# Retention with increments from the last chunk down, and output gates multiplied on GpSimd during the attention

## The chip, the cores and the metric

The kernel runs on one core of a Trainium2 chip. The metric is the device time of one execution in microseconds, as the median of several runs. The engines are named as the profile names them: PE (TensorE matmuls and transposes; PEld are its weight loads), DVE (VectorE), ACT (ScalarE), POOL (GpSimd), and SP (SyncE), whose queue issues nearly all DMA transfers. Each engine works through a queue of its own in order and waits on semaphores for the others.

## What is computed

One inference step of a trunk of two layers over 1024 latent tokens and 256 context tokens, in float32, model width 1024. Each layer normalises and modulates the tokens, multiplies them with one input projection, and splits the result among three mixers and a gate path: bidirectional retention (4 heads, chunks of 128 tokens), grouped-query attention (6 heads), latent attention (6 heads). The mixers' outputs are joined, multiplied by SiLU of the gate, and go through the output projection into a gated residual:

```python
def step(s, inp):
    qi, ki, vi = inp
    a = jnp.einsum('bihd,bjhd->bhij', qi, ki) * intra
    o = (jnp.einsum('bhij,bjhe->bihe', a, vi)
         + jnp.einsum('bihd,bhde->bihe', qi, s) * q_dec[None, :, :, None])
    s = s * c_dec[None, :, None, None] + jnp.einsum('bjhd,bjhe->bhde', ki * k_dec[None, :, :, None], vi)
    return s, o

o_f, s_f = retention_chunkwise(q, k, v, log_g[0], s0_f)
o_b, s_b = retention_chunkwise(jnp.flip(q, 1), jnp.flip(k, 1), jnp.flip(v, 1), log_g[1], s0_b)
o = rms_norm(o_f + jnp.flip(o_b, 1))

y = jnp.concatenate([o_ret, o_gqa, o_mla], axis=-1) * jax.nn.silu(z_gate)
return x + g_res * (y @ w_out)
```

## The kernel before

The tokens are ten tiles of 128, eight latent (t = 0 to 7) and two context (8, 9). Matrix products with weights run as three matmuls each, on operands split into a high and a low part: wh and wl for weights (split on POOL, L195 and L196, from `raw`), ah and al for activations (`split_x`: ACT writes ah, L407, DVE subtracts it for al, L408). A layer goes through these stages:

- The input projection, in column blocks.
- The gate stage `z_blk` (L686 to L688): the last 1024 columns, transposed, with SiLU as tanh on ACT and (th + 1) z on DVE (`eo`, L693); the factor one half is left for later. Its results go to DRAM, `s_gT`, a row for each gate column. Between its matmul groups a generator `aside()` is stepped, which does the latents' keys and values, the retention, and the attention's preparation.
- The retention, over chunks. First, with t going up, `increments`: kd, the keys times the decay (two DVE multiplies, L804), four matmuls (L809), the forward state S[0:64] advanced on DVE (L816, L817), the backward increments copied by ACT into S[64:128]. Then a sweep over the tiles from the last to the first on DVE advances the backward state (L840, L841) and stores it (L842). Then three pipelined steps for each tile: `stage_a` multiplies q by the decay (qd, two DVE multiplies, L855), transposes it (L858), q and k (L864 and the line after), and copies them from PSUM (qdT and the block diagonal BD on ACT, kT on DVE, L869); `stage_b` is two matmuls (L875) and a multiply by the decay mask (At, L877); `stage_c` is eight matmuls (L884, L885), a norm, and a multiply into yx (L891).
- The attention (class `Attention`), in 60 passes a layer, each of a head pair's 256 queries. Scores (L1215, L1216, and for latent heads L1218), exponentials on ACT, transposes (L1256) with pT split by ACT (L1260) and DVE (L1261), products with V (L1272, L1273). POOL makes the query tiles Qg, Qm, Qr (L1137, L1139) and splits K and V; each `y_job`, 30 a layer, spreads the reciprocal sums on POOL (rb, L1303), transposes them on PE (L1306) and multiplies the heads on DVE (L1307).
- The output projection `phase_d`: for each tile `gated` transposes the retention's output (L1423), multiplies it and the heads by the gates and one half on DVE (L1424, L1425), reloads x into yx and splits the product; then 24 matmuls for each tile and column block of 256 (L259 to L261), the multiply by the residual gate (eg, L1451) and the residual add on POOL (L1453). Only the first of the four column blocks has `gated` in it.

Tiles are rotating buffers (`bufs=`): a new one waits until the readers of the old are done. The order on each engine is set by the program's text, by the generators' yields, and by a scheduler that places the instructions; `pin` holds an instruction in its place. Names: yx, the tokens' wide buffers, first q and head queries, then mixer outputs, then x; `gt`, the loaded gates; S, the retention states; cur and fin, the sweep's states; st and kpr, staged and final latent keys.

Of the kernel before, what the change touches and what calls it, by code (L numbers as in the profile page):

```python
# [10 lines left out]
F32 = mybir.dt.float32  # L11
# [9 lines left out]
NL = 8  # L21
# [56 lines left out]
RW = 1  # L78
PINV = 0
PINT = 0  # L80
# [4 lines left out]
def hybrid_trunk(tc, I, O):  # L85
# [315 lines left out]
    def pool_copy(o, i):  # L401
        G.tensor_scalar(o, i, 1.0, 1.0, op0=ALU.mult, op1=ALU.mult)
# [41 lines left out]
    def phase_b(l, p1, acts, ws, first, first_side, first_done, att):  # L444
# [267 lines left out]
        def aside():  # L712
# [30 lines left out]
    cdec_all = cst.tile([P, DEPTH, 4], F32, name="cdec")  # L743

# [8 lines left out]
    def decays(tmp):  # L753
# [22 lines left out]
        A.activation(cdec_all[0:64], lg_all[0:64, :, 0, :], AF.Exp, scale=128.0)  # L776
        A.activation(cdec_all[64:128], lg_all[64:128, :, 1, :], AF.Exp, scale=128.0)

    def retention(l, rt):
        if True:  # L780
            lg, dec, cdec = lg_all[:, l], dec_all[:, l], cdec_all[:, l]
            MT = rt.tile([P, 4, 128], F32, name="MT")
            dma(MT.rearrange("p h c -> p (h c)"), s_mt[l])

            def bc(ap, lo=0, hi=P):
                return ap.unsqueeze(2).to_broadcast([hi - lo, 4, 64])

            def h4(ap):
                return ap.rearrange("p (h d) -> p h d", h=4)

            S = rt.tile([P, NT, 256], F32, name="S")
            dma(S[0:64, 0, :].rearrange("p (h e) -> p h e", h=4), I["state_ret"][0, l, 0].rearrange("h d e -> d h e"))
            V.memset(S[0:64, NL, :], 0.0)
            fin = rt.tile([P, 256], F32, name="fin")

            def load(t):
                kv = rt.tile([P, 512], F32, name="kv", tag="kv", bufs=3)
                dma(kv, s_rkv[l][rows(t), :])
                return kv

            def increments(t, kv):
                kd = rt.tile([P, 4, 2, 64], F32, name="kd", tag="kd", bufs=1)
                for d in range(2):
                    i = V.tensor_tensor(kd[:, :, d, :], h4(kv[:, 0:256]), bc(dec[:, 2 + d, :]), op=ALU.mult)  # L804
                    if PINV and d == 0:
                        pin(i)
                ps = bank("m")
                for h in range(4):
                    i = T.matmul(ps[:, h * 64:(h + 1) * 64], kd[:, h, :, :].rearrange("p a b -> p (a b)"),  # L809
                             kv[:, 256 + h * 64:256 + (h + 1) * 64], start=True, stop=True)  # L810
                    if PINT and h == 0:
                        pin(i)

                if t != NL - 1:
                    nxt = S[0:64, t + 1, :] if t != NT - 1 else fin[0:64, :]
                    V.tensor_tensor(h4(nxt), h4(S[0:64, t, :]), bc(cdec[0:64, :], 0, 64), op=ALU.mult)  # L816
                    V.tensor_tensor(nxt, nxt, ps[0:64, :256], op=ALU.add)  # L817

                A.copy(S[64:128, t, :], ps[64:128, :256])

            kv = load(0)
            for _ in range(RW):
                yield
            for t in range(NT):
                yield
                nx_kv = load(t + 1) if t + 1 < NT else None
                increments(t, kv)
                kv = nx_kv
            for seq in (range(NL - 1, -1, -1), range(NT - 1, NL - 1, -1)):
                cur = rt.tile([P, 256], F32, name="cur", tag="cur", bufs=2)  # L830
                if seq[-1] == 0:
                    dma(cur[64:128, :].rearrange("p (h e) -> p h e", h=4), I["state_ret"][0, l, 1].rearrange("h d e -> d h e"))
                else:
                    V.memset(cur[64:128, :], 0.0)
                for t in seq:
                    last = t == seq[-1]
                    nx = None
# [6 lines left out]
                yield  # L844
            for d in range(2):
                dma(new_state[0, l, d].rearrange("h d e -> d h e"), fin[64 * d:64 * d + 64, :].rearrange("p (h e) -> p h e", h=4))

            BD = rt.tile([P, 2, 256], F32, name="BD")
            V.memset(BD, 0.0)

            def stage_a(t, kv):
                q = yx[t][:, 0:256]
                qd = rt.tile([P, 4, 2, 64], F32, name="qd", tag="kd", bufs=1)
                for d in range(2):
                    V.tensor_tensor(qd[:, :, d, :], h4(q), bc(dec[:, d, :]), op=ALU.mult)  # L855
                pt = bank("tp")
                for h in range(4):
# [4 lines left out]
                for j in range(2):  # L862
                    T.transpose(pt[:, j * 128:(j + 1) * 128], q[:, j * 128:(j + 1) * 128], ident)
                    T.transpose(pt[:, 256 + j * 128:256 + (j + 1) * 128], kv[:, j * 128:(j + 1) * 128], ident)  # L864
                pq = pt[:, 0:256].rearrange("p (j c) -> p j c", j=2)
                A.copy(BD[0:64, :, 0:128], pq[0:64])
                A.copy(BD[64:128, :, 128:256], pq[64:128])
# [785 lines left out]
```

## Time and profile before

| | before |
|---|---|
| median of 3 runs | 2179.33 us (2175.82 to 2180.6) |
| the profiled execution | 2173.39 us, span 2171.6 us |
| PE busy | 2095.2 us, 96% |
| DVE / ACT / POOL busy | 71% / 54% / 41% |
| retention, layer 0 / 1 | about 375 to 505 us / 1415 to 1550 us |
| attention, layer 0 / 1 | about 510 to 995 us / 1552 to 2040 us |
| output projection, layer 0 / 1 | about 996 to 1110 us / 2041 to 2168 us |

A line of groups reads: line, engine, operation, output from inputs, shapes, count, then busy time and the mean of one in ns, then the idle time of that engine just before these instructions and what ended it. A line of stretches gives its bounds and length, then the busy time and, in brackets, the number of instructions of PE, PEld, DVE, ACT and POOL in this order (or of PE alone where only PE was asked for), the clock granted to PE as a share of full speed, the share of DMA time, and GB/s.

### The profile page before, as it was taken

The page shows a single profiled execution, that of the slowest core. Times are in us where ns is not written, and L with a number is a line of the kernel's source. Part 1 is how long each engine was busy: PE and PEld are TensorE (multiplying, and loading weights), DVE is VectorE, ACT ScalarE, POOL GpSimd, SP SyncE. Part 2 cuts the span into 40 slices and gives each one's busy share as a digit, 9 for nine tenths or more (in the row PEclk, how much of TensorE's full clock was granted, in tenths as well). Part 3 has the DMA queues.
Part 4 walks back from the last instruction along what each step waited for, and adds up shares of the span by engine and source line. Part 5 has one row for each costly group of instructions (what it writes and reads, how often), then busy time and mean ns, then how long its engine had stood idle before and what let it go on. Part 6 is the DMA issues. An engine that isn't in the chain of part 4 may idle for free.

```text
span 2171.6 us, 42095 instructions
## 1 busy us (share of the span) xinstructions
PE 2095.2 (96%) x14928; PEld 1878.0 (86%) x14928; DVE 1546.4 (71%) x3982; ACT 1182.8 (54%) x3151; POOL 891.9 (41%) x1322
## 2 busy tenths in 40 slices
PE   6999999999999999998999999999999999999998
PEld 3899987787888888887999999888788888888898
DVE  4625683667989999998174358566699899999834
ACT  4503233226888888885253233313488888888523
POOL 2341242106475455423543224230465645544374
PEclk9999999999999999999999999999999999999999
DMA  9542436413010000026143112452301000000532
GB/s 323 144 140 61 127 110 197 122 49 99 12 39 17 11 22 16 10 63 179 49 153 105 46 58 52 152 151 71 91 23 27 17 22 22 16 5 18 178 95 98
DMA packets 196954, 173.15 MB, mean 80 GB/s; under 512 B 34968, under 2 KB 179208, under 8 KB 196744
## 3 DMA queue, kind: packets, MB, share of 16 engines
q1 hardware_dynamic: 195304, 165.21, 25.7%
q10 hardware_dynamic: 1440, 5.24, 0.6%
q8 instruction: 119, 1.95, 0.4%
q14 instruction: 91, 0.75, 0.1%
HBM read 124.64 MB, written 45.76 MB: 78 GB/s over the span
## 4 chain that ended last, share of the span: by engine, by line
PE 68%; DVE 7%; DMA 3%; ACT 3%; POOL 2%; issue 2%; SPq 0%; DVEq 0%; ACTq 0%; POOLq 0%
PE tp L1256 11%; PE acc L1215 6%; PE o L1272 6%; PE o L1273 6%; PE acc L1216 6%; PE acc L260 5%; PE acc L261 5%; PE acc L259 5%; PE acc L1218 3%; PE acc L686 2%; PE acc L687 2%; PE acc L688 2%; DMA gt<-s_gT 1%; DVE al L408 1%; PE o L884 1%
## 5 line engine op out<-in xcount | busy, mean ns | idle before, releaser
L261 PE MATMUL acc<-wh,al 128*128 128x256 f32 (+1 forms) x1760 | 502.0, 285 | 8.3 <-DVE al L408 8.2
L259 PE MATMUL acc<-wh,ah 128*128 128x256 f32 (+1 forms) x1760 | 505.1, 287 | 0.5 <-ACT ah L407 0.4
L260 PE MATMUL acc<-wl,ah 128*128 128x256 f32 (+1 forms) x1760 | 503.4, 286 | 0.0
L1224 DVE TENSOR_REDUCE nm<-acc 128x1 f32<-128x512 f32 (+1 forms) x624 | 412.2, 666 | 40.6 <-PE acc L1218 23.2
L1261 DVE TENSOR_TENSOR pT<-tp,pT 128x512 fp32r<-128x512 f32 (+1 forms) x624 | 413.3, 664 | 32.3 <-ACT pT L1260 27.1
L1238 ACT ACTIVATE pn<-acc,nm 128x512 f32<-128x512 f32 (+1 forms) x624 | 421.4, 681 | 20.0 <-DVE nm L1229 17.5
L1260 ACT CAST pT<-tp 128x512 fp32r<-128x512 f32 (+1 forms) x624 | 356.2, 573 | 138.4 <-PE tp L1256 131.9
L1256 PE MATMUL tp<-ident,pn 128*128 128x128 f32 x2400 | 424.5, 274 | 4.6 <-DVE pT L1261 3.1
L259 PEld LDWEIGHTS acc<-wh,ah 128*128 128x128 f32 x1760 | 335.9, 191 | 12.9 <-issue 8.2
L261 PEld LDWEIGHTS acc<-wh,al 128*128 128x128 f32 x1760 | 332.7, 189 | 12.6 <-DVE al L408 12.1
L260 PEld LDWEIGHTS acc<-wl,ah 128*128 128x128 f32 x1760 | 335.1, 190 | 0.8 <-issue 0.8
L1272 PE MATMUL o<-pT,V 128*128 128x256 f32 x1200 | 325.0, 293 | 0.8 <-DVE yx L1285 0.7
L1256 PEld LDWEIGHTS tp<-ident,pn 128*128 128x128 f32 x2400 | 288.3, 141 | 36.0 <-PE tp L1256 5.8
L1273 PE MATMUL o<-pT,V 128*128 128x256 f32 x1200 | 314.1, 284 | 0.0
L1272 PEld LDWEIGHTS o<-pT,V 128*128 128x128 f32 x1200 | 226.6, 189 | 19.7 <-DVE yx L1285 5.7
L1273 PEld LDWEIGHTS o<-pT,V 128*128 128x128 f32 x1200 | 226.5, 189 | 16.2
L195 POOL TENSOR_SCALAR wh<-raw 128x512 fp32r<-128x512 f32 (+2 forms) x144 | 83.7, 591 | 335.3 <-PE acc L261 142.9
L196 POOL TENSOR_TENSOR wl<-raw,wh 128x512 fp32r<-128x512 f32 (+2 forms) x144 | 164.5, 1153 | 5.0
L1137 POOL TENSOR_SCALAR Qm<-yx 64x256 fp32r<-64x256 f32 x120 | 48.5, 404 | 231.9 <-PE acc L1216 225.2
L686 PE MATMUL acc<-ah,wh 128*128 128x512 f32 (+1 forms) x384 | 142.6, 371 | 0.0
L1215 PE MATMUL acc<-K,Qm 128*128 128x512 f32 (+1 forms) x312 | 140.4, 450 | 1.0
L688 PE MATMUL acc<-al,wh 128*128 128x512 f32 (+1 forms) x384 | 139.7, 364 | 0.0
(278 smaller groups left out, 3972.6 us busy)
## 6 DMA issues: line engine op xcount, KB each, us to landing
raw<-in_w_ada_dram SPq DMA_DIRECT2D x96, 256.0 KB, 3.2
raw<-in_w_in_dram SPq DMA_DIRECT2D x56, 256.0 KB, 3.1
s_gT<-eo SPq DMA_DIRECT2D x80, 128.0 KB, 2.5
kv<-s_rkv SPq DMA_DIRECT2D x40, 256.0 KB, 2.9
gt<-s_gT SPq DMA_DIRECT2D x20, 512.0 KB, 5.1
yx<-in_x_sample_dram SPq DMA_DIRECT2D x16, 512.0 KB, 8.6
raw<-in_w_in_dram SPq DMA_DIRECT2D x56, 128.0 KB, 2.4
raw<-in_w_out_dram SPq DMA_DIRECT2D x48, 128.0 KB, 2.9
```

The lines of the kernel that those rows point to most:

```text
L259: T.matmul(ps, ah[:, k, :], wh, start=(k == 0), stop=False)
L260: T.matmul(ps, ah[:, k, :], wl, start=False, stop=False)
L261: T.matmul(ps, al[:, k, :], wh, start=False, stop=(k == KC - 1))
L686: T.matmul(ps, wh, ah[:, k, :], start=(k == 0), stop=False)
L1215: T.matmul(ps, p.Q[:, 0, qs], K, start=True, stop=False)
L1224: V.tensor_reduce(nm[:, b:b + 1], ps, axis=AX.X, op=ALU.max, negate=True)
L1238: A.activation(pn, ps, AF.Exp, bias=p.ng[i], accum_out=p.su[:, i, b:b + 1])
L1256: T.transpose(pt[:, c * 128:(c + 1) * 128], pn[:, c * 128:(c + 1) * 128], ident)
L1260: A.copy(ph, p3)
L1261: V.tensor_tensor(pl, p3, ph.bitcast(F32), op=ALU.subtract)
L1272: T.matmul(p.po, vc, p.gran[b][:, 0, c, :], start=(ch == 0), stop=False)
L1273: T.matmul(p.po, vc, p.gran[b][:, 1, c, :], start=False, stop=(ch == last))
```

## The change

- Retention: the increments run with t going down, the kv tiles of 9 and the next two are loaded before the latents, and the backward state is advanced at once on DVE (`advanced`). The sweep is gone. ACT copies the forward increments, and POOL advances the forward state in `stage_a`. kd is one instruction. q is not multiplied before its transposes: POOL writes it twice side by side (`doubled`, qq), and one DVE multiply by a transposed decay table, decT, empties the bank (qdT); the two extra transposes of q fall away. kT is copied by ACT. The output is transposed in the new `stage_d`.
- Attention: the gates of a head pair and two tiles are loaded when its first half is done (30 loads a layer, 128 KB each, and five of 256 KB for the retention's rows), and POOL multiplies the heads and the retention's output by them in `y_job`.
- `phase_d`: no gate loads, multiplies or transposes; `gated` splits yx and reloads x. One half goes into the residual gate (`ada_gate`).
- Buffers: kd and At share three buffers with qq, cn has three instead of four, ukv shares one, and the attention has four `gt` and one `gr`.

```diff
-        V.tensor_copy(row[:16, :], ps[:16, :128])
+        V.tensor_scalar(row[:16, :], ps[:16, :128], 0.5, None, op0=ALU.mult)
...
-        G.tensor_scalar(o, i, 1.0, 1.0, op0=ALU.mult, op1=ALU.mult)
+        return G.tensor_scalar(o, i, 1.0, 1.0, op0=ALU.mult, op1=ALU.mult)
...
-            with tc.tile_pool(name=f"lt{l}", reuse_waits="tile", bufs=1, side="right") as lt:
-                yield from grouped(latents(l, lt), LG)
-            with tc.tile_pool(name=f"rt{l}", reuse_waits="tile", bufs=1, side="right") as rt:
-                yield from retention(l, rt)
+            with tc.tile_pool(name=f"kv{l}", reuse_waits="tile", bufs=1, side="right") as kvp:
+                load = kv_loader(l, kvp)
+                kv = load(NT - 1)
+                with tc.tile_pool(name=f"lt{l}", reuse_waits="tile", bufs=1, side="right") as lt:
+                    yield from grouped(latents(l, lt), LG)
+                with tc.tile_pool(name=f"rt{l}", reuse_waits="tile", bufs=1, side="right") as rt:
+                    yield from retention(l, rt, load, kv)
...
+        def advanced(eng, d, nxt, cur, inc=None):
+            if inc is not None:
+                eng.tensor_tensor(h4(nxt), h4(cur), bc(cdec[d], d.start, d.stop), op=ALU.mult)
+                eng.tensor_tensor(nxt, nxt, inc, op=ALU.add)
+            else:
+                st = rt.tile([P, 256], F32, name="cur", tag="cur", bufs=2)[d]
+                pin(eng.tensor_tensor(h4(st), h4(cur), bc(cdec[d], d.start, d.stop), op=ALU.mult))
+                eng.tensor_tensor(nxt, nxt, st, op=ALU.add)
+        def increments(t, kv):
+            kd = rt.tile([P, 4, 2, 64], F32, name="kd", tag="kd", bufs=3)
+            V.tensor_tensor(kd, h4(kv[:, 0:256]).unsqueeze(2).to_broadcast([P, 4, 2, 64]),
+                            dec[:, 2:4, :].rearrange("p a h -> p h a").unsqueeze(3).to_broadcast([P, 4, 2, 64]), op=ALU.mult)
+            ps = bank("m")
+            for h in range(4):
+                T.matmul(ps[:, h * 64:(h + 1) * 64], kd[:, h, :, :].rearrange("p a b -> p (a b)"),
+                         kv[:, 256 + h * 64:256 + (h + 1) * 64], start=True, stop=True)
+            if t not in (0, NL, NT - 1):
+                advanced(V, B, S[B, t - 1, :], S[B, t, :], ps[B, :256])
+            elif t == NL:
+                advanced(V, B, fin[B, :], S[B, t, :], ps[B, :256])
+            elif t == NT - 1:
+                V.tensor_copy(S[B, t - 1, :], ps[B, :256])
+            if t != NL - 1:
+                A.copy(S[F, t + 1, :] if t != NT - 1 else fin[F, :], ps[F, :256])
...
+        def doubled(t):
+            if t < NT:
+                qqs[t] = rt.tile([P, 4, 2, 64], F32, name="qq", tag="kd", bufs=3)
+                pin(pool_copy(qqs[t], h4(yx[t][:, 0:256]).unsqueeze(2).to_broadcast([P, 4, 2, 64])))
+        for t in range(NT - 1, -1, -1):
+            yield
+            nx_kv = load(t - 1) if t else load(0)
+            increments(t, kv)
+            if t < 2:
+                doubled(1 - t)
+            kv = nx_kv
...
+            if t >= 3:
+                stage_d(t - 3, outs.pop(t - 3), pk[:, 256:512])
+            qdT = rt.tile([P, 4, 128], F32, name="qdT", tag="qdT", bufs=2)
+            V.tensor_tensor(qdT.rearrange("p h c -> p (h c)"), pt, decT.rearrange("p h c -> p (h c)"), op=ALU.mult)
+            pq = pt.rearrange("p (j x c) -> p x j c", j=2, x=2)
+            A.copy(BD[0:64, :, 0:128], pq[0:64, 0])
+            A.copy(BD[64:128, :, 128:256], pq[64:128, 1])
+            kT = rt.tile([P, 2, 128], F32, name="kT", tag="kT", bufs=1)
+            A.copy(kT.rearrange("p j c -> p (j c)"), pk[:, 0:256])
+            if t < NL - 1:
+                advanced(G, F, S[F, t + 1, :], S[F, t, :])
+            elif t == NL:
+                advanced(G, F, fin[F, :], S[F, NT - 1, :])
...
+        def stage_d(t, o, pt):
+            for i in range(2):
+                T.transpose(pt[:, i * 128:(i + 1) * 128], o[:, i * 128:(i + 1) * 128], ident)
+            A.copy(yx[t][:, 0:256], pt)
...
-                    i = V.tensor_tensor(kd[:, :, d, :], h4(kv[:, 0:256]), bc(dec[:, 2 + d, :]), op=ALU.mult)
...
-            for seq in (range(NL - 1, -1, -1), range(NT - 1, NL - 1, -1)):
...
-                    if not (last and t == 0):
-                        nx = fin if last else rt.tile([P, 256], F32, name="cur", tag="cur", bufs=2)
-                        V.tensor_tensor(h4(nx[64:128, :]), h4(cur[64:128, :]), bc(cdec[64:128, :], 0, 64), op=ALU.mult)
-                        V.tensor_tensor(nx[64:128, :], nx[64:128, :], S[64:128, t, :], op=ALU.add)
-                    V.tensor_copy(S[64:128, t, :], cur[64:128, :])
-                    cur = nx
...
-                q = yx[t][:, 0:256]
-                qd = rt.tile([P, 4, 2, 64], F32, name="qd", tag="kd", bufs=1)
-                for d in range(2):
-                    V.tensor_tensor(qd[:, :, d, :], h4(q), bc(dec[:, d, :]), op=ALU.mult)
-                pt = bank("tp")
-                for h in range(4):
-                    T.transpose(pt[:, h * 128:(h + 1) * 128], qd[:, h, :, :].rearrange("p a b -> p (a b)"), ident)
-                qdT = rt.tile([P, 4, 128], F32, name="qdT", tag="qdT", bufs=2)
-                A.copy(qdT.rearrange("p h c -> p (h c)"), pt)
-                pt = bank("tp")
...
-                V.tensor_copy(kT.rearrange("p j c -> p (j c)"), pt[:, 256:512])
...
-                if halves[p.i, p.pr] == 2:
+                if halves[p.i, p.pr] == 1:
+                    load_gates(p)
+                else:
...
+        def load_gates(p):
+            gates[p.i, p.pr] = g = at.tile([P, 2, 128], F32, name="gt", tag="gt", bufs=LEAD + 1)
+            dma(g, s_gT[l][(2 + p.i) * P:(3 + p.i) * P, 2 * p.pr * P:(2 * p.pr + 2) * P].rearrange("p (t c) -> p t c", t=2))
+        rets = []
+        def gate_retention(p):
+            if rets:
+                pr, g = rets.pop()
+                c = yxs[:, 2 * pr:2 * pr + 2, 0:Y_H].rearrange("p t (k c) -> p k t c", k=2)
+                G.tensor_tensor(c, c, g, op=ALU.mult)
+            if p.i == 1:
+                rets.append((p.pr, at.tile([P, 2, 2, 128], F32, name="gr", tag="gr", bufs=1)))
+                dma(rets[0][1].rearrange("p k t c -> p k (t c)"),
+                    s_gT[l][0:Y_H, 2 * p.pr * P:(2 * p.pr + 2) * P].rearrange("(k p) c -> p k c", p=P))
...
+            G.tensor_tensor(head_cols(p), head_cols(p), gates.pop((p.i, p.pr)), op=ALU.mult)
+            gate_retention(p)
...
-            def load_g(t):
-                g = pg.tile([P, D], F32, name="gt", tag="gt", bufs=3)
-                dma(g.rearrange("p (k c) -> p k c", c=128), s_gT[l].rearrange("(k p) t -> p k t", p=P)[:, :, rows(t)])
-                return g
-            gts = {t: load_g(t) for t in range(2)}
             def gated(t):
-                gt = gts.pop(t)
-                pt = bank("tp")[:, :Y_H]
-                for i in range(2):
-                    T.transpose(pt[:, i * 128:(i + 1) * 128], yx[t][:, i * 128:(i + 1) * 128], ident)
-                V.scalar_tensor_tensor(gt[:, Y_H:], yx[t][:, Y_H:], 0.5, gt[:, Y_H:], op0=ALU.mult, op1=ALU.mult)
-                V.scalar_tensor_tensor(gt[:, :Y_H], pt, 0.5, gt[:, :Y_H], op0=ALU.mult, op1=ALU.mult)
+                n = 2 if t == 0 else 4
+                for k in range(0, KC, n):
+                    split_x(yx[t], act_of(acts, t), k, k + n)
                 dma(yx[t], x_src(l, t))
-                if t + 2 < NT:
-                    gts[t + 2] = load_g(t + 2)
-                for k in range(0, KC, 4):
-                    split_x(gt, act_of(acts, t), k, k + 4)
```

In DVE's queue of layer 0, before, at the end of the retention's sweep (S, cur and fin are the states, kT the transposed keys of tile 0):

```order
L840 TENSOR_TENSOR cur<-cur,cdec 64x256
L841 TENSOR_TENSOR cur<-cur,S 64x256
L855 TENSOR_TENSOR qd<-yx,dec 128x4x64
L842 COPY S<-cur 64x256
L840 TENSOR_TENSOR fin<-cur,cdec 64x256
L855 TENSOR_TENSOR qd<-yx,dec 128x4x64
L841 TENSOR_TENSOR fin<-fin,S 64x256
L869 COPY kT<-tp 128x256
```

The same queue at the same place after the change, at the end of the increments:

```order
L821 TENSOR_TENSOR S<-S,cdec 64x256
L822 TENSOR_TENSOR S<-S,tp 64x256
L690 SCALAR_TENSOR_TENSOR eo<-th,acc 128x256 x4
L830 TENSOR_TENSOR kd<-kv,dec 128x512
L875 TENSOR_TENSOR qdT<-tp,decT 128x512
L690 SCALAR_TENSOR_TENSOR eo<-th,acc 128x256
L895 TENSOR_TENSOR At<-tp,MT 128x512
```

No sweep stands between the last kd and tile 0's operations, and kT has left the queue.

PE in layer 0 at the attention's first scores, before (L686 to L688 are the gate stage):

```order
L686 MATMUL acc<-ah_128,wh 128x512
L687 MATMUL acc<-ah_128,wl 128x512
L688 MATMUL acc<-al_129,wh 128x512
L1215 MATMUL acc<-K,Q_6438 128x512 x3
L686 MATMUL acc<-ah_130,wh 128x256
L687 MATMUL acc<-ah_130,wl 128x256
```

After, where the scores are L1247 and L1248 and the gate stage L683 to L685:

```order
L684 MATMUL acc<-ah_127,wl 128x512
L685 MATMUL acc<-al_128,wh 128x512
L1247 MATMUL acc<-K,Q_6394 128x512 x3
L683 MATMUL acc<-ah_129,wh 128x512
L684 MATMUL acc<-ah_129,wl 128x512
L685 MATMUL acc<-al_130,wh 128x512
L683 MATMUL acc<-ah_129,wh 128x512
L1248 MATMUL acc<-K,Q_6394 128x512 x3
```

The first scores stand one group of gate matmuls earlier: a 512-wide group follows them where only the last, 256-wide one did.

DVE in layer 0 from the attention's end into the output projection, before:

```order
L1307 TENSOR_TENSOR yx<-yx,tp 128x2x128
L1425 SCALAR_TENSOR_TENSOR gt<-tp,gt 128x256
L1285 TENSOR_TENSOR yx<-o,o_13632 64x2x128
L1425 SCALAR_TENSOR_TENSOR gt<-tp,gt 128x256
L1307 TENSOR_TENSOR yx<-yx,tp 128x2x128
L408 TENSOR_TENSOR al_13647<-gt,ah_13646 128x4x128 x4
L1425 SCALAR_TENSOR_TENSOR gt<-tp,gt 128x256
L408 TENSOR_TENSOR al_13647<-gt,ah_13646 128x4x128
```

After:

```order
L1317 TENSOR_TENSOR yx<-o,o_13712 64x2x128
L1359 TENSOR_TENSOR yx<-yx,tp 128x2x128
L1317 TENSOR_TENSOR yx<-o,o_13727 64x2x128
L1359 TENSOR_TENSOR yx<-yx,tp 128x2x128
L405 TENSOR_TENSOR al_13743<-yx,ah_13742 128x2x128 x4
L405 TENSOR_TENSOR al_13743<-yx,ah_13742 128x4x128 x3
L1491 TENSOR_TENSOR eg<-acc,gate 128x256
```

The gate multiplies between the heads' last multiplies and the first subtractions are gone, and tile 0 is split in four smaller pieces.

## Rows read from the trace of the kernel before

**Rows 1.** The page's parts 1 and 5: the engines, and one group of DVE.

```profile
PE 2095.2 (96%) x14928; PEld 1878.0 (86%) x14928; DVE 1546.4 (71%) x3982; ACT 1182.8 (54%) x3151; POOL 891.9 (41%) x1322
...
L1261 DVE TENSOR_TENSOR pT<-tp,pT 128x512 fp32r<-128x512 f32 (+1 forms) x624 | 413.3, 664 | 32.3 <-ACT pT L1260 27.1
```

**Rows 2.** Stretches of 40 us in layer 0's attention and at its end.

```profile
600.00:640.00 40.00, 39.89 (x280) 35.52 (x278) 37.03 (x79) 34.17 (x88) 29.08 (x43) 1.00 0.16 42
...
960.00:1000.00 40.00, 36.42 (x258) 31.82 (x257) 34.98 (x69) 27.82 (x70) 10.28 (x12) 1.00 0.35 100
```

**Rows 3.** Stretches of 10 us, layer 0, retention and the attention's first scores.

```profile
380.00:390.00 10.00, 8.30 (x46) 7.60 (x47) 4.99 (x15) 1.88 (x5) 0.00 (x0) 0.83 0.61 173
...
410.00:420.00 10.00, 8.85 (x52) 7.39 (x51) 9.46 (x20) 2.37 (x7) 9.67 (x15) 1.00 0.33 98
420.00:430.00 10.00, 7.53 (x29) 6.22 (x29) 5.16 (x12) 1.71 (x4) 0.77 (x2) 0.66 0.27 80
...
510.00:520.00 10.00, 7.35 (x39) 6.32 (x38) 7.89 (x14) 4.84 (x13) 4.44 (x8) 0.83 0.60 170
```

**Rows 4.** Waits of PE in layer 0, then layer 1: total, times, longest.

```profile
PE tp L875 <- DVE kT L869: 3.6, 1, 3.6
PE tp L809 <- DVE kd L804: 2.2, 1, 2.2
...
PE acc L1215 <- DVE eo L693: 2.6, 1, 2.6
...
PE tp L809 <- DVE kd L804: 2.7, 1, 2.7
PE tp L875 <- DVE kT L869: 0.9, 1, 0.9
...
PE acc L1215 <- DVE eo L693: 3.8, 1, 3.8
...
PE tp L1306 <- POOL rb L1303: 2.1, 1, 2.1
```

**Rows 5.** The chain in layer 0's retention: start, duration, what.

```profile
376.61 4.21 DMA kv<-s_rkv
...
416.38 1.13 DVE S L842 x2
...
420.19 0.86 DVE fin L840
...
422.00 0.44 DVE kT L869
```

**Rows 6.** Groups of POOL over the whole run, by shape.

```profile
L1137 POOL TENSOR_SCALAR Qm<-yx 64x256 fp32r<-64x256 f32 x120 | 48.5, 404 | 231.9 <-PE acc L1216 225.2
...
L1453 POOL TENSOR_TENSOR yx<-yx,eg 128x256 f32<-128x256 f32 x60 | 46.5, 776 | 55.3 <-DVE eg L1451 55.0
```

**Rows 7.** PE alone: the projection's first column block against the next stretch.

```profile
996.50:1033.30 36.80, 33.29 (x259) 1.00 0.90 264
1033.30:1070.10 36.80, 36.80 (x311) 1.00 0.20 58
2041.20:2078.70 37.50, 33.11 (x259) 1.00 0.86 264
2078.70:2116.20 37.50, 37.50 (x318) 1.00 0.12 36
```

**Rows 8.** The chain in layer 0's output projection.

```profile
1019.66 6.92 DMA gt<-s_gT
```

**Rows 9.** Groups of DVE in 996 to 1034 us, by shape.

```profile
L408 DVE TENSOR_TENSOR al<-gt,ah 128x512 fp32r<-128x512 f32 x20 | 18.6, 951 | 1.7 <-ACT ah L407 1.6
L1424 DVE SCALAR_TENSOR_TENSOR gt<-yx,gt 128x768 f32<-128x768 f32 x7 | 6.7, 953 | 2.2 <-DMA gt<-s_gT 2.2
...
L1425 DVE SCALAR_TENSOR_TENSOR gt<-tp,gt 128x256 f32<-128x256 f32 x9 | 3.7, 414 | 0.1
```

**Rows 10.** Line L408 over the whole run: count, then least, median and longest ns.

```profile
L408 DVE TENSOR_TENSOR al<-gt,ah x40: 677/1016/1777, 996.5 to 2073.9; 128x512 fp32r<-128x512 f32 x40
```

More of the change, by code (lines that the diff above doesn't have):

```diff
@@ L77 @@
 SV = 0
-RW = 1
-PINV = 0
-PINT = 0
 WG = 1
@@ L743, in hybrid_trunk @@
     cdec_all = cst.tile([P, DEPTH, 4], F32, name="cdec")
+    lgT_all = cst.tile([P, DEPTH, 4], F32, name="lgT")
     def decay_loads(pool):
@@ L775, in decays @@
         V.tensor_scalar(dec_all[:, :, 2:4, :], dec_all[:, :, 2:4, :], 0.125, None, op0=ALU.mult)
[L776 to L802, printed above, removed]
-                for d in range(2):
-                    i = V.tensor_tensor(kd[:, :, d, :], h4(kv[:, 0:256]), bc(dec[:, 2 + d, :]), op=ALU.mult)
-                    if PINV and d == 0:
-                        pin(i)
-                ps = bank("m")
-                for h in range(4):
[L809 to L825, printed above, removed]
@@ L826, in retention @@
                 nx_kv = load(t + 1) if t + 1 < NT else None
-                increments(t, kv)
+                if t:
+                    doubled(t + 1)
+                st[t] = stage_a(t, kv, qqs.pop(t))
                 kv = nx_kv
-            for seq in (range(NL - 1, -1, -1), range(NT - 1, NL - 1, -1)):
[L830 to L837, printed above, removed]
-                    if not (last and t == 0):
-                        nx = fin if last else rt.tile([P, 256], F32, name="cur", tag="cur", bufs=2)
-                        V.tensor_tensor(h4(nx[64:128, :]), h4(cur[64:128, :]), bc(cdec[64:128, :], 0, 64), op=ALU.mult)
-                        V.tensor_tensor(nx[64:128, :], nx[64:128, :], S[64:128, t, :], op=ALU.add)
-                    V.tensor_copy(S[64:128, t, :], cur[64:128, :])
-                    cur = nx
-                yield
@@ L845, in retention @@
-            for d in range(2):
[L846 to L851, printed above, removed]
-                q = yx[t][:, 0:256]
-                qd = rt.tile([P, 4, 2, 64], F32, name="qd", tag="kd", bufs=1)
-                for d in range(2):
-                    V.tensor_tensor(qd[:, :, d, :], h4(q), bc(dec[:, d, :]), op=ALU.mult)
-                pt = bank("tp")
-                for h in range(4):
-                    T.transpose(pt[:, h * 128:(h + 1) * 128], qd[:, h, :, :].rearrange("p a b -> p (a b)"), ident)
-                qdT = rt.tile([P, 4, 128], F32, name="qdT", tag="qdT", bufs=2)
-                A.copy(qdT.rearrange("p h c -> p (h c)"), pt)
-                pt = bank("tp")
[L862 to L867, printed above, removed]
-                kT = rt.tile([P, 2, 128], F32, name="kT", tag="kT", bufs=1)
-                V.tensor_copy(kT.rearrange("p j c -> p (j c)"), pt[:, 256:512])
-                return kv, qdT, kT
@@ L893, in retention @@
-            st, At = {}, {}
-            kv = load(0)
-            for t in range(NT + 2):
-                yield
-                if t >= 2:
-                    stage_c(t - 2, st[t - 2][0], st[t - 2][1], At.pop(t - 2))
-                if 1 <= t <= NT:
-                    At[t - 1] = stage_b(st[t - 1][2])
-                if t < NT:
-                    nx_kv = load(t + 1) if t + 1 < NT else None
-                    st[t] = stage_a(t, kv)
-                    kv = nx_kv
+            elif t >= 3:
+                stage_d(t - 3, outs.pop(t - 3), bank("tp")[:, :256])
@@ L927, in latents, with load @@
     def latents(l, lt):
-        raw = lt.tile([P, 6, 2, 64], F32, name="ukv")
-        dma(raw.rearrange("p h a d -> p (h a d)"), I["w_ukv"][l])
-        cns = []
-        for b in range(0, NCH, 4):
+        raw = lt.tile([P, 6, 2, 2, 64], F32, name="ukv", tag="sv", bufs=1)[:, :, 0]
+        dma(raw, I["w_ukv"][l].rearrange("p (h a d) -> p h a d", h=6, a=2))
+        def load(b):
             m = min(4, NCH - b)
-            cn = lt.tile([P, 4, 128], F32, name="cn", tag="cn", bufs=4)
+            cn = lt.tile([P, 4, 128], F32, name="cn", tag="cn", bufs=3)
             src = I["cache_mla_ckv"][0, l] if b == 0 else s_kv[l][(b - 4) * P:(b - 4 + m) * P, 128:256]
             dma(cn[:, :m, :], src.rearrange("(c p) d -> p c d", p=P))
-            cns.append((b, m, cn))
+            return b, m, cn
+        cns = [load(b) for b in range(0, NCH - 4, 4)]
         u = [lt.tile([P, 6, 64], F32R, name=f"u{i}") for i in range(4)]
@@ L956, in latents @@
         nxt = transposed(*cns[0])
+        cns.append(load(12))
         for x in range(len(cns)):
```

93 lines of the change are left out of this document (73 added, 20 removed).

## The prediction

> **What bounds the kernel now.** I read the page's first part first: TensorE (PE) is busy 96% of the span, VectorE (DVE) 71%, ScalarE (ACT) 54%, GpSimd (POOL) 41% [rows 1]. A share of the whole says nothing about a stage, so next came the table by stretches of 40 us. In the attention of layer 0 PE is busy 39.9 of 40 us with the clock at 1.00, beside DVE at 37 and POOL at 29, the most that POOL has in a stretch from 560 to 960 us; the stretch at the attention's end, 960:1000, has 36.4 [rows 2]. So nothing can be won inside the attention by relieving another engine; something can only be lost. The third view, in stretches of 10 us before the attention, shows PE with holes, each with a granted clock of 0.83 or less [rows 3], and the waits of PE name their causes [rows 4].
>
> So the kernel is a full PE stream with three kinds of holes in each layer: in the retention, at the attention's first scores, and from the attention's end through the first column block of the out-projection. The change touches all three, and I cost them hole by hole.
>
> **Retention.** In layer 0 PE waits 2.2 us for kd L804 and 3.6 us for kT L869 [rows 4]. Behind the first is a kv load of 4.21 us. Behind the second is DVE's own queue: the sweep's S L842 and fin L840 (0.86 us) stand ahead of kT [rows 5], and DVE is busy 9.46 of 10 us in 410:420 [rows 3]. Each hole is followed by PE at the lower of its two clock levels (1.2 of 2.4 GHz). 380:390 at 0.83 lost 10 x 0.17 = 1.7 us of work. 420:430 at 0.66 lost 3.4 us, less half of the 2.5 us that PE was idle in it: 2.2 us. Layer 0 has 2.2 + 1.7 + 3.6 + 2.2 = 9.7 us in this. Layer 1 waits 2.7 and 0.9 us [rows 4]; with one drop as in 380:390 that is 5.3 us. Together 15.0 us is the most that can come back.
>
> The change removes both causes. kv of tiles 9, 8 and 7 is loaded before the latents, so the first kd waits for no transfer. The sweep's 28 DVE instructions a layer (0.57 us each by S L842 [rows 5]) go; the backward state takes the two DVE instructions a tile that the forward state had. The two qd multiplies a tile and the kT copy (0.44 us each, by kT's row, all 128x256) leave DVE for one 128x512 multiply with an operand in PSUM, 0.66 us as pT L1261 [rows 1]. kd becomes one instruction of 128x512 for two of 128x256, which I count even. Per tile DVE saves 2.8 x 0.57 + 3 x 0.44 - 0.66 = 2.3 us, 23 us a layer, and only the part at the hole is on the path. PE keeps its count: eight transposes a tile before and after.
>
> What it adds: POOL doubles q (128x512, at most 0.81 us, twice Qm L1137) and advances the forward state (two operations of 64x256, at most 0.78 us each by yx L1453) [rows 6], 2.4 us a tile. POOL had nothing to do in 380:390 and 0.77 of 10 in 420:430 [rows 3], so there is room for them; but they stand in one queue with the weight splits, which wait until PE frees wh. ACT takes the kT copy and one copy of the output; it is under 2.5 of 10 busy in 380 to 430 [rows 3], which hides them. The later kv loads (up to 4.21 us each [rows 5]) now follow one another closely, and the first three tiles' stages stand close together with few gate matmuls between. So I count two thirds, 10 us; the bounds are 0 and 15. A loss isn't excluded: one stage that waits for POOL opens a hole like that of kd, 2.2 us and 1.7 us of clock, 4 us.
>
> **The attention's first scores.** PE waits 2.6 and 3.8 us before L1215 [rows 4]; with the clock at 0.83 in 510:520 [rows 3], and the same in layer 1, it is 2.6 + 1.7 + 3.8 + 1.7 = 9.8 us. The order before leaves 24 matmuls of 128x256 of the gate stage behind the first scores; after it, a whole 512-wide group stands there as well (24 more of twice 0.118 us, worked out below: 5.7 us of cover). The releaser is in DVE's queue, which is shorter by the sweep. But the scores also need kpr and Q, which come by loads and copies of their own, and that cover is used up if these are late. I take half, 5 us; the bounds are 0 and 9.8.
>
> **Gates during the attention.** A layer's 30 multiplies of 128x256 (0.78 us each by yx L1453 [rows 6], the same shape and operands in SBUF) and five of 128x512 (at most twice that) go onto POOL: 30 x 0.78 + 5 x 1.56 = 31 us in 480 us, 2.6 in 40. Beside 29 of 40 at most [rows 2] PE's stream hides this: I count nothing. If that cover goes, it is the second rival below. The 35 loads stand on SP between those of K, V and q; a gate load waits until POOL frees one of four buffers, and the loads behind it wait with it, with four jobs of slack. The DMA share there is 0.16 [rows 2].
>
> **Out-projection.** In 996.5:1033.3 PE did 259 matmuls, of them 16 of the transposes that go; in the next 36.8 us, 311. Layer 1 did 259 against 318 in 37.5 us [rows 7]; I take 16 there too. At 36.8 / 311 = 0.118 us each the work missing is (311 - 243) x 0.118 = 8.0 us and (318 - 243) x 0.118 = 8.9 us; four more transposes a layer lie outside, 0.9 us in all: 17.8 us. Two causes are seen. The chain goes over gt loads, one of 6.92 us [rows 8]. And DVE had for each tile 0.95 us of gt L1424, 0.41 of gt L1425, twice 0.95 of al L408 [rows 9] and 0.42 of eg, 3.7 us, against 24 x 0.118 = 2.8 us of PE. After the change no gate load and no gt multiply is left there; DVE has 2 x 0.95 + 0.42 = 2.3 us a tile, or 2.5 at al's median of 1.02 [rows 10], and PE is the bound. The x load stays and has DMA to itself. I take all 17.8; the lower bound is nothing, where al takes its longest, 1.78 us [rows 10]: 2 x 1.78 + 0.42 = 4.0 us a tile. Before the first al, at the attention's end, one gt L1424 and two gt L1425 stand in DVE's queue; 0.95 + 2 x 0.41 = 1.8 us a layer, bounds 0 and 3.5 (960:1000 is 3.5 us under 600:640 [rows 2]). 17.8 + 3.6 makes 21 us; the bounds are 0 and 25.
>
> The trace shows al, with both operands in SBUF, between 0.68 and 1.78 us [rows 10], and pT L1261, with one in PSUM, at 0.66 on average [rows 1] beside a POOL that is busy most of the time. The Trainium skill, "SBUF — State Buffer", section "Who interferes with whom", states that a DVE instruction with two SBUF inputs contends with a GpSimd instruction that reads SBUF, and that whichever issues first keeps the port for the whole instruction. By that rule the gates on POOL can't stretch the attention's pT, and its row agrees; the rule speaks against the out-projection's al beside POOL's residual adds, which is the third rival.
>
> **Sum.** 10 + 5 + 21 = 36 us. The profiled execution took 2173.4 us (span 2171.6, 1.8 around it), which makes 2137.4 on its scale. It lies 5.9 us under the median of the runs; against that, 2179.3 - 36 = 2143 us.
>
> **Rivals.**
> 1. Only the out-projection gains: the holes before the attention move, since POOL's doubling stands behind splits that wait for PE, and the scores wait for kpr. For it: the holes are ended by late inputs too, a kv load for one [rows 5]. Against: POOL's idle stretches [rows 3]. 2179.3 - 21 = 2158 us. Chance 0.20.
> 2. POOL becomes the attention's bound, and the kernel is slower. A gate waits in POOL's in-order queue for DVE's product, which waits for PE's transposes; behind it stand Q and K splits and the next rb. PE waited for rb L1303 already, 2.1 us in layer 1's attention [rows 4]. There are 60 such jobs; with w us of PE wait for each, the time is 2143 + 60 w: from w = 0.6 the gain is gone, and w = 1 gives 2203 us. Against: Qm L1137 stood idle 225 us, waiting for PE to free its buffer [rows 6], so POOL runs ahead. Chance 0.08.
> 3. al at its longest, with DVE still the bound of the out-projection's first block: 2143 + 18 = 2161 us. Against: the median of 1.02, with POOL's adds already beside it [rows 10]. Chance 0.07.
> 4. The waits only change their names (x loads for gt loads, kpr for eo, POOL for kT) and the kernel is within 4 us of 2179. Chance 0.05.
>
> **How the numbers follow.** The forecast has 0.60. With all terms whole, 15.0 + 9.8 + 25 = 50 us, it is 2129; with the out-projection's half and nothing else, 2169. I take 2128 to 2171, which holds the first and the third rival and leaves out the second and fourth, 0.13. Under 0.2% (4.4 us) a difference can't be told from none. Faster 0.87, the same 0.05, slower 0.08.
>
> **What would show it.** Right: no PE wait for kd or kT and a clock of 1.00 in the retention; 300 or more matmuls in the out-projection's first 37 us; PE at 39.8 of 40 in the attention with POOL no more than 32. Wrong: PE waits on rb, Qm or K in many jobs; PE waits for qdT or BD behind qq; al near 1.8 us. The forecast falls first if the attention's stream is broken, since 60 small waits outweigh every hole above.

## The result, and the profile after

The changed kernel takes 2163.05 us (median of four runs, 2160.97 to 2163.72) against 2177.57 for the kernel before in the same runs: a ratio of 0.994, 95% interval 0.9922 to 0.9957, or 14.5 us between the medians (the ratio alone makes it 13). It is faster, as forecast, and inside the range, but the gain is 14.5 of the 36 us that the sum gave. The profiled executions took 2162.85 and 2173.39 us.

First the page of the kernel after: the engines and the groups that answer [rows 1].

```profile
PE 2084.2 (96%) x14888; PEld 1870.0 (87%) x14888; DVE 1502.0 (70%) x3830; ACT 1183.5 (55%) x3180; POOL 978.2 (45%) x1444
...
L1293 DVE TENSOR_TENSOR pT<-tp,pT 128x512 fp32r<-128x512 f32 (+1 forms) x624 | 413.2, 664 | 36.1 <-ACT pT L1292 30.6
```

DVE lost 44 us of work and POOL took on 86, while pT is as long as before. Neither says where the time went. The stages do. The table is worked out from the first and last matmuls of each stage in the profiled executions; the first column runs from the first gate-stage matmul to the last product with V (retention, first scores and attention), the second from there to the next layer's gate stage, or to the end.

| us | layer 0: gate stage to end of attention | out-projection and next in-projection | layer 1: gate stage to end of attention | out-projection to end |
|---|---|---|---|---|
| before | 675.0 | 374.4 | 670.3 | 132.5 |
| after | 678.0 | 367.7 | 670.2 | 125.0 |
| forecast of the change | -9 | -10 | -6 | -11 |
| measured | +3.0 | -6.7 | -0.1 | -7.5 |

So the out-projection gave 14.2 of the 21 us, and the retention, the first scores and the attention together lost 2.9. (1.7 of the 14.2 is a stretch at the lower clock near 1131 us, in the next in-projection, that only the kernel before had.) Waits of PE in the kernel after, layer 0, from 376 to 520 us (total, times, longest), against the first three lines of [rows 4]:

```profile
PE o L903 <- DVE oret L910: 4.3, 5, 1.2
PE tp L868 <- POOL qq L399: 1.3, 1, 1.3
PE tp L871 <- DVE At L895: 0.9, 1, 0.9
PE acc L1247 <- DVE eo L690: 0.7, 1, 0.7
```

kT is gone from the list, kd is down to 0.2 us, and the first scores wait 0.7 us for eo instead of 2.6. In their place PE waits before the output matmuls of five of the ten tiles, for oret, the instruction that empties the previous tile's PSUM bank. Two 10 us stretches of the retention still run partly at the lower clock level, where [rows 3] had them at 380 and 420:

```profile
440.00:450.00 10.00, 10.00 (x63) 9.04 (x63) 6.34 (x22) 2.89 (x9) 2.03 (x4) 0.83 0.19 44
480.00:490.00 10.00, 9.10 (x53) 8.52 (x54) 4.71 (x21) 1.88 (x5) 0.00 (x0) 0.83 0.15 49
```

The waits of PE in the two attentions, layer 0 (560 to 960) and then layer 1 (1600 to 2000). Before there was one in each, 1.7 us in layer 0 and the last line of [rows 4] in layer 1:

```profile
PE tp L1358 <- POOL rb L1355: 5.4, 2, 3.2
...
PE tp L1358 <- POOL rb L1355: 4.2, 2, 2.9
```

And the out-projection, to be read beside [rows 7]: the first column block and the stretch behind it, then the block in pieces of 5 us (a matmul on a bound counts on both sides), then what PE waited for in it.

```profile
999.30:1036.10 36.80, 35.68 (x291) 1.00 0.58 188
1036.10:1072.90 36.80, 36.80 (x312) 1.00 0.15 42
...
999.30:1004.30 5.00, 3.89 (x27) 1.00 0.01 3
1004.30:1009.30 5.00, 4.99 (x40) 1.00 0.73 227
1009.30:1014.30 5.00, 5.00 (x45) 1.00 0.75 261
1014.30:1019.30 5.00, 5.00 (x44) 1.00 0.93 300
...
L258 PE MATMUL acc<-wh,al 128*128 128x256 f32 x99 | 28.4, 287 | 1.1 <-DVE al L405 1.1
```

From the third tile on PE does 44 matmuls in 5 us, its full rate. All that is still missing, 21 matmuls or 2.5 us, is missing in the first 10 us, where PE waits twice for al, 1.1 us together.

### The profile page after: what moved, and what is told of

Its sections match the earlier page's. It is cut to its first block, busy times and chain, and to the rows that moved or that the text cites. A ratio compares the mean times of both kernels' runs of the same rounds, so it can differ in the third digit from the quotient of the medians.

```text
span 2161.1 us, 42292 instructions
## 1 busy us (share of the span) xinstructions
PE 2084.2 (96%) x14888; PEld 1870.0 (87%) x14888; DVE 1502.0 (70%) x3830; ACT 1183.5 (55%) x3180; POOL 978.2 (45%) x1444
## 5 line engine op out<-in xcount | busy, mean ns | idle before, releaser
L193 POOL TENSOR_TENSOR wl<-raw,wh 128x512 fp32r<-128x512 f32 (+2 forms) x144 | 164.7, 1155 | 5.2
L1247 PE MATMUL acc<-K,Qm 128*128 128x512 f32 (+1 forms) x312 | 140.6, 451 | 1.0
L683 PE MATMUL acc<-ah,wh 128*128 128x512 f32 (+1 forms) x384 | 141.4, 368 | 0.0
L684 PE MATMUL acc<-ah,wl 128*128 128x512 f32 (+1 forms) x384 | 139.8, 364 | 0.0
L685 PE MATMUL acc<-al,wh 128*128 128x512 f32 (+1 forms) x384 | 139.5, 363 | 0.0
```

Of the source, the lines that this page charges most:

```text
L193: G.tensor_tensor(wl, raw, wh.bitcast(F32), op=ALU.subtract)
L1247: T.matmul(ps, p.Q[:, 0, qs], K, start=True, stop=False)
```

## The experiments

Ratios are to the kernel before on the same chip, with 95% intervals. My theory after reading the trace was that the retention's loop hangs on one chain: all tiles' outputs use one PSUM bank, `o`, and the next tile's output matmuls wait until the last has been squared (ACT), summed, normalised in a dozen small DVE instructions (Newton) and multiplied out. The first rival was that the gates on POOL ate a real gain. The first four runs part the change and test both.

**The retention alone.** `gated` loads and multiplies the gates as before, without transposes:

```diff
+            V.tensor_tensor(gt[:, Y_H:], yx[t][:, Y_H:], gt[:, Y_H:], op=ALU.mult)
+            V.tensor_tensor(gt[:, :Y_H], yx[t][:, :Y_H], gt[:, :Y_H], op=ALU.mult)
...
-            G.tensor_tensor(head_cols(p), head_cols(p), gates.pop((p.i, p.pr)), op=ALU.mult)
-            gate_retention(p)
```

> The changed kernel with its retention, but with the gates back in the out-projection: loaded there (512 KB a tile) and multiplied by two DVE instructions a tile; the retention's output stays transposed, so no transposes return. Theory (the retention gained nothing because its loop is bounded by the chain from one tile's output matmuls through square, reduce, Newton steps and the multiply that frees the one PSUM bank 'o'): the waits of PE for oret stay at 0.6 to 1.2 us on most tiles, the waits for rb go back to one of 1.7 to 2.1 us a layer, the out-projection loses 5 to 6 us a layer again; about 2167 us, 10 under the kernel before. Rival (the gates on POOL ate a gain of 15 us that the retention and the first scores had): 2156 us or less.

Measured: 0.9992 (0.9983 to 1.0002). The retention and the earlier scores alone are worth nothing that can be measured. oret is waited for as in the whole change (5.0 us in layer 0, longest 1.2). That is 0.5 us under the kernel before on this chip, where the theory had 10 and the rival 21 or more: the theory's cause, the waits for oret, is seen, but I had put the retention's worth too high even so.

**The gates alone**, on the kernel before, whose retention gets the output transposes:

```diff
+            def stage_d(t, o):
+                pt = bank("tp")[:, :256]
+                for i in range(2):
+                    T.transpose(pt[:, i * 128:(i + 1) * 128], o[:, i * 128:(i + 1) * 128], ident)
+                A.copy(yx[t][:, 0:256], pt)
...
+            G.tensor_tensor(head_cols(p), head_cols(p), gates.pop((p.i, p.pr)), op=ALU.mult)
+            gate_retention(p)
```

> The kernel before with its retention (increments up, sweep, q multiplied on DVE), but with the output transposed there, the gates loaded and multiplied on POOL in the attention, and the out-projection that only splits. Theory: the out-projection gives 12 to 14 us in both layers, rb's waits take 5 to 7 us of it; kd and kT are waited for as before: about 2171 us. Rival (the whole gain is the out-projection's and the gates cost nothing): 2163 us, as the whole change.

Measured: 1.0051 (1.0034 to 1.0068), slower, and both expectations missed. The out-projections gained 6.6 and 7.7 us as in the whole change, but the stage before them lost 14.0 and 10.4. Waits of PE from 515 to 960 us in this run:

```profile
PE tp L1337 <- POOL rb L1334: 7.2, 2, 4.2
PE acc L1225 <- ACT pn L1248: 5.4, 1, 5.4
```

So the two halves of the change are not additive: nothing and +11 us make -13.

**Two banks.** Odd tiles' outputs go to the rotating tag, so that a tile no longer waits for the one before:

```diff
-            bo = bank("o")
+            bo = bank("m" if t % 2 else "o")
```

> The changed kernel, with the retention's output of odd tiles in a bank of the rotating tag 'tp' and of even tiles in 'o', so that a tile's output matmuls no longer wait until the tile before has left its bank. Theory (the one bank and the norm chain bound the loop): the waits for oret (5 us a layer) go, and with them the two stretches at half clock in layer 0; 2163 - 12 = 2151 us, 2148 to 2156. Rival (PE has no other work to put there, or the wait moves to At or qq): 2160 to 2165 us.

Measured: 0.9892 (0.9875 to 0.9908), 2151.31 us, as the theory said, about 10 us under the change. What is left of oret in layer 0 from 376 to 512 us is a single wait in front of a transpose:

```profile
PE tp L868 <- POOL qq L399: 1.3, 1, 1.3
PE tp L916 <- DVE oret L910: 1.0, 1, 1.0
```

**Without the multiplies on POOL.** This kernel loads the gates and leaves the product with them out; only its time is of use.

```diff
-                G.tensor_tensor(c, c, g, op=ALU.mult)
...
-            G.tensor_tensor(head_cols(p), head_cols(p), gates.pop((p.i, p.pr)), op=ALU.mult)
+            gates.pop((p.i, p.pr))
```

> The changed kernel without POOL's gate multiplies (30 and 5 a layer left out; the gate loads stay). Theory (the multiplies stand in POOL's queue ahead of rb, and PE waits): the first wait for rb of each layer (2.2 and 1.3 us) goes, the second falls from 3.2 and 2.9 to 1.7 and 2.1 us, and one stretch at half clock goes: 2163 - 7 = 2156 us. Rival (POOL's 30 us a layer are hidden, and the rb waits come from elsewhere): 2162 to 2164 us.

Measured: 0.9917 (0.9903 to 0.9932) where the change has 0.994; 5 us, with intervals that overlap. The profile is plainer than the time: the first wait for rb is gone and the second is back at 1.7 and 2.1 us. In layer 0:

```profile
PE tp L1357 <- POOL rb L1354: 1.7, 1, 1.7
```

**What the bank is worth elsewhere.** The same edit on the kernel before, and on the retention alone:

> The kernel before with its retention's output in two banks in turn. Theory (its norm chain of 4.7 us was just covered by gate matmuls, waits of 0.1 us; its holes are kd, kT and the first scores, and those stay): ratio 0.998 to 1.0. Rival (the bank alone is worth the 10 us, with either retention): 0.995.

> The changed retention with two banks, with the gates in the out-projection (e1 with the banks). Theory (once the bank doesn't bound it, the new retention and the earlier first scores bring the 10 to 15 us that were forecast): ratio 0.994 to 0.996. Rival (they bring nothing without the gates' change): 0.999.

Measured: 0.9972 (0.9963 to 0.9982) and 0.9937 (0.9922 to 0.9952). The kernel before gains 6 us, between the two expectations: its loop hung on the bank too. No wait of PE over 0.2 us shows it, since gate matmuls fill the time; the weight loads do. At its output matmuls (L884) the trace of before has 17 waits for L891, the multiply that empties the bank, 6.6 us together over both layers and nearly all of them of PEld; with two banks it has none, and a tile's period falls from 6.60 to 6.31 us. With two banks the new retention is worth 7.6 us over the old one (2173.9 x (0.9972 - 0.9937)), with one bank 1.7, which can't be told from nothing.

**The chain itself.** Why did the new retention's chain hold the bank longer? Worked out from the traces, from the start of a tile's last output matmul to the end of its multiply, the chain takes 4.85 us on average before and 5.21 after. Most of the difference lies in a layer's first two tiles (in layer 0 7.4 and 5.9 us against 5.3 and 5.3); the other eight take 4.9 against 4.7. DVE after, one tile (start, duration, instruction; the idle time before it and its releaser in brackets):

```profile
450.36 0.22 DVE L150 TENSOR_SCALAR nwx<-ss 128x4 f32<-128x4 f32 x1
450.61 0.17 DVE L151 TENSOR_SCALAR nwu<-nwx 128x4 int32<-128x4 int32 x1
450.82 0.58 DVE L152 TENSOR_SCALAR nwy<-nwu 128x4 int32<-128x4 int32 x1
451.31 0.16 DVE L153 TENSOR_SCALAR nwx<-nwx 128x4 f32<-128x4 f32 x1
```

POOL in the same microseconds:

```profile
449.94 0.61 POOL L825 TENSOR_TENSOR cur<-S,cdec 64x256 f32<-64x256 f32 x1 [0.53 <-POOL qq L399]
450.63 0.74 POOL L826 TENSOR_TENSOR S<-S,cur 64x256 f32<-64x256 f32 x1
```

An instruction on four columns takes 0.58 us instead of 0.17 and ends with POOL's add. L152 runs 20 times, once for each tile and layer: eight times it takes 0.58 to 0.65 us, each time beside a POOL instruction with two inputs (six of them the state's), and twelve times 0.15 to 0.17. In layer 0's first tile, where POOL comes to the state late, behind weight splits, six Newton steps are stretched. The next run moves the forward state from POOL to DVE:

```diff
-                advanced(G, F, S[F, t + 1, :], S[F, t, :])
+                advanced(V, F, S[F, t + 1, :], S[F, t, :])
```

> The changed kernel with the forward state advanced on DVE in the retention's last loop, not on POOL. Theory (the norm chain that holds the one bank is lengthened by POOL: L152, 0.17 us alone, takes 0.59 while POOL's add of the state runs): the waits for oret fall from 0.6 to 1.2 us to 0.2 to 0.7, 3 to 5 us gained in all, ratio 0.992. Rival (DVE's queue is what lengthens the chain, by qdT ahead of the Newton steps, and two more instructions of 0.4 us a tile lengthen it further): waits for oret of 1 us and more, ratio 0.996 or more.

Measured: 0.9892 (0.9869 to 0.9914), 2150.17 us: more than expected, as much as two banks give. DVE has two more instructions of 0.41 us a tile, and the chain is shorter, 4.65 us on average. The sixth tile's instructions in this run (those above are the fifth's), and the waits of PE from 376 to 515 us:

```profile
451.15 0.17 DVE L151 TENSOR_SCALAR nwu<-nwx 128x4 int32<-128x4 int32 x1
451.36 0.17 DVE L152 TENSOR_SCALAR nwy<-nwu 128x4 int32<-128x4 int32 x1
451.44 0.16 DVE L153 TENSOR_SCALAR nwx<-nwx 128x4 f32<-128x4 f32 x1
```

```profile
PE o L903 <- DVE oret L910: 1.6, 2, 1.4
...
PE tp L868 <- POOL qq L399: 0.7, 1, 0.7
```

**POOL's queue in the attention.** rb, the spread of the reciprocal sums, is written by ACT:

```diff
-            G.tensor_scalar(rb.rearrange("p (x c) -> p x c", c=64), ri.unsqueeze(2).to_broadcast([P, 4, 64]), 1.0, 1.0,
-                            op0=ALU.mult, op1=ALU.mult)
+            A.copy(rb.rearrange("p (x c) -> p x c", c=64), ri.unsqueeze(2).to_broadcast([P, 4, 64]))
```

> The changed kernel, one bank as it is, with rb written by ACT instead of POOL. Theory (POOL's queue ahead of rb costs the changed kernel 5.4 and 4.2 us of PE waits and one stretch at half clock): no PE wait on rb over 0.5 us; 9 to 11 us gained, ratio 0.989 to 0.990 where the change has 0.994. Rival (ACT's 11 us a layer come back as waits on pT or pn): 0.992 or more.

> The gates' change alone on the kernel before (as e2), with rb written by ACT. e2 was at 1.005, though its out-projection gained 14 us. Theory (its PE waits for rb, 7.2 and 8.0 us with five stretches at half clock, are the same queue of POOL): 14 to 20 us under e2, ratio 0.996 to 0.9985; the first scores' waits of 5.4 and 4.4 us stay. Rival (the loss is the first scores' and the longer retention's, and rb only shows it): 1.001 or more.

> The changed kernel with the two banks for the retention's output, and the spread of the reciprocal sums (rb, 30 a layer) on ACT instead of POOL. Theory (rb stands behind gates and V splits in POOL's queue; with two banks PE waited 1.3 + 4.3 + 1.8 + 2.8 us for it and ran two stretches of 6.8 us at half clock): these go, ratio to the kernel before 0.983 to 0.985, 11 to 14 us under the run with two banks alone. Rival (ACT, at 33 to 34 of 40 us in the attention, is delayed by 11 us more a layer and passes that on to pT): ratio 0.989 or more.

Measured: on the change 0.9916 (0.9889 to 0.9942), the wait for rb gone from the list of 560 to 960 us, the gain less clear than expected, since the interval reaches the change's own; on the gates alone 0.9968 (0.9955 to 0.998) instead of 1.0051, so rb's place in POOL's queue cost that run 18 us (the kernel before, too, waits 1.7 and 2.1 us for rb); with two banks 0.9851 (0.9836 to 0.9865), 2139.98 us, another 9 us under two banks alone. POOL in the change, layer 0, just before the longer wait ends at 648.0 us:

```profile
644.00 1.14 POOL L193 TENSOR_TENSOR V<-st,V 128x448 fp32r<-128x448 f32 x1
645.10 0.73 POOL L1360 TENSOR_TENSOR yx<-yx,gt 128x256 f32<-128x256 f32 x1
645.79 0.57 POOL L192 TENSOR_SCALAR V<-st 128x448 fp32r<-128x448 f32 x1
646.44 1.13 POOL L193 TENSOR_TENSOR V<-st,V 128x448 fp32r<-128x448 f32 x1
647.53 0.41 POOL L1355 TENSOR_SCALAR rb<-ri 128x256 f32<-128x256 f32 x1
```

A gate multiply stands among V's splits in front of rb, without a gap. The earlier wait has another cause, seen in the waits of POOL from 548 to 566 us: the gates of the retention have a single buffer, and their multiplies wait in the queue for its loads.

```profile
POOL yx L1344 <- DMA gr<-s_gT: 8.3, 3, 2.9
```

**The out-projection's adds on DVE**, for the third rival:

```diff
-                    (V if c == 3 else G).tensor_tensor(xc, xc, e, op=ALU.add)
+                    (V if c in (0, 3) else G).tensor_tensor(xc, xc, e, op=ALU.add)
```

> The changed kernel with the residual adds of the out-projection's first column block on DVE instead of POOL (ten a layer). Theory (POOL's adds beside al lengthen al, 0.99 us on average where it takes 0.68 alone, and cost the first tiles): al's mean falls under 0.85 us, PE does 295 matmuls or more in the block's first 36.8 us instead of 291, 1 to 3 us gained, ratio 0.993. Rival (DVE has 0.43 us more a tile, and PE was the bound already): the same 291 or fewer, ratio 0.994 to 0.996.

Measured: 0.9953 (0.9936 to 0.9969), not to be told from the change. al of 128x512 falls from 990 to 868 ns on average, and the block's first 36.8 us hold 292 matmuls where the change has 291. POOL's adds do lengthen al, and that doesn't matter, since PE is the bound by then. The run doesn't settle the rival, though: al is slowest in the second tile, 1.78 us for each of its two pieces beside POOL's weight splits (L193), in this run as in the change, and PE waits 0.7 us for the first of them. Splits on another engine weren't tried.

**All three edits together** (two banks, state on DVE, rb on ACT):

> The changed kernel with all three edits: two banks, rb on ACT, the forward state advanced on DVE. Two banks and the state on DVE each gave about 10 to 13 us. Theory (both cure the same thing, the chain that holds the bank): together with rb no more than two banks and rb on ACT have, ratio 0.983 to 0.986. Rival (they cure two things and add): 0.980 or less.

Measured: 0.9847 (0.9823 to 0.987), 2139.57 us, the same as without the state on DVE. Two banks and the shorter chain cure one thing. It and the run with two banks and rb on ACT beat both kernels, by 33 us the one before.

## Why the prediction was wrong

**Retention and first scores, 15 us.** The holes closed as forecast: over both layers PE's waits for kd, kT and eo fell from 15.8 to 1.6 us. But 15.4 us of new ones opened in the retention: oret 9.6, qq 2.3, At 1.8, small ones 1.7. The step that failed is "POOL had nothing to do, so there is room for them", with the one before it, that DVE's saving is on the path only at the hole. I costed POOL's and DVE's work by busy time; the loop is bounded by latency, a chain of some 5 us for each tile around a single bank, and the trace of before hid it under gate matmuls. The new work lengthened that chain by 0.36 us a tile, because POOL's state runs beside the Newton steps. qdT in front of them isn't the cause: with the state on DVE it still stands there, and the chain is 4.65 us, shorter than before. Nor was POOL idle where the loop's first tile came to lie: [rows 3] has it at 9.67 of 10 us in 410:420, in the kernel after it is 9.92, and that tile's chain is the longest, 7.4 us. The gain came back as waits; with the state on DVE alone the kernel is at 0.9892, some 10 us under the change. The lower clock cost less than before, not more: by the granted clock (10 us at 0.83 are 1.7 us lost), 5.1 us against 6.8 in layer 0's stage, nothing against 3.4 in layer 1's. With the bank doubled the new retention alone stands 13.7 us under the kernel before (2173.9 x 0.0063), near the 15; but 6 of these the bank gives to the old retention too.

The rule of the Trainium skill that I used ("SBUF — State Buffer", "Who interferes with whom") was weighed in the wrong place. The out-projection's al is stretched, and it costs 0.7 us a layer; the small Newton instructions are stretched, and they were on the path. The same section says that a single-source `tensor_scalar` may take both ports and then contend with GpSimd; L152 at 0.58 instead of 0.17 us beside POOL agrees.

**Gates, nothing.** The term was put at nothing, and rb's waits grew from 1.7 and 2.1 us to 5.4 and 4.2, 5.8 us in all; the run without the multiplies says about 5 us, with intervals that overlap. The second rival named the mechanism and its place, but as 60 small waits; it was two in each layer, where POOL's queue is full of K and V splits or waits for gr's loads. "Beside 29 of 40 at most" was an average over 40 us; the queue in front of rb was full without a gap.

**Out-projection, 21 us.** The mechanism held, the size was off: 14.2. PE reaches its full rate from the third tile. I took the full rate for the first two as well, and the first starts up on the first pieces of ah and al, the second on an al stretched by the weight splits, which costs the 2.5 us a layer above. The tail gave 1.6 us a layer where I had 1.8: from the last product with V to the first matmul on al, 3.64 us before and 2.05 after.

**Rivals.** The first, only the out-projection gains, came nearest (2158 forecast, 2163 measured), and the cause it named for the retention, POOL, had its part: mostly by the chain, and by the weight splits too, behind which qq stood when PE waited for it (1.3 and 1.0 us). The third, al at its longest, held for the second tile alone.

**Open.** Why the gates cost 24 us before the out-projection on the old retention and some 5 on the new one is only partly shown: 18 us go with rb; the first scores' waits of 5.4 and 4.4 us stayed when rb moved. That they come from the one more step in front of the attention's preparation wasn't tried. Nor were two buffers for gr. That the earlier wait for rb comes from gr's loads is read from the queue alone.

## What to carry to other kernels

A stage in which PE looks full may still be bounded by a chain, if other matmuls fill it: look at the waits of the weight loads, follow one buffer from its writer to the instruction that frees it, and compare that time with the loop's period, before counting busy time. Work moved to an idle engine is free only if nothing short on the critical chain is stretched by it, and nothing urgent stands behind it in its queue. Halves of a change that are worth 0 and -11 us alone can be worth +13 together, so test them together as well as apart.

## What the hardware showed

A DVE instruction on 128x4 took 0.58 us where it takes 0.17 alone, while POOL's 64x256 add of 0.74 us ran: it ended with POOL's instruction, whatever its own size. In the changed kernel the granted clock was at its lower level for part of 440:450 (0.83) after four PE waits of 1.3, 0.7, 0.9 and 1.1 us at 420, 425, 432 and 440 us, none of them as long as the 2 to 4 us waits that it followed in the kernel before. The same four waits in layer 1 (1.0, 0.7, 0.9, 1.1 us) were followed by no such stretch (1.00 from 1450 to 1530), and neither was the 3.2 us wait for rb that ends at 648.0 us (1.00 in 640:660). So the length of a wait alone did not decide it.
